# A two-layer fp32 encoder trunk on one Trainium2 core: the first feed-forward stage's down projection by seven products, its results added to x by transfers of 768 KB

## The chip, the core and the metric

The kernel runs on one core of one Trainium2 chip. Its engines are named here as the profile names them: PE is TensorE (PEld its weight loads), DVE is VectorE, ACT is ScalarE, POOL is GpSimd, SP is SyncE, which issues most loads. What counts is the device time of one execution in microseconds (us), as the median of several runs on the chip.

## The reference

Two sequences, a prompt of 512 tokens and a sample of 256, each token 1024 wide in fp32, go through a trunk of two layers. Each layer is a feed-forward block, a mixer and a second feed-forward block, each added to x after an RMS norm. The mixer of the first layer is an S5 state space (32 groups of 16 channels, 64 states, both directions) beside a neighbourhood attention, that of the second a windowed attention with grouped keys. The feed-forward block is

```python
def swiglu(x, wg, wu, wd):
    return (jax.nn.silu(x @ wg) * (x @ wu)) @ wd
```

with a hidden width of 2816, so 22 blocks of 128. The result is x after the last block, added with half weight per feed-forward block.

## The kernel before

**Stages.** `Trunk.run` goes through six stages: feed-forward 0, the mixer of layer 0, feed-forward 1 and 2, the mixer of layer 1, feed-forward 3. The 768 tokens lie in SBUF as six tiles of 128 x 1024 (`self.x`, in the order `TILES`, two of the sample and four of the prompt). Every fp32 operand of a matmul is split into a high and a low part (`split`, L86 to L90: ScalarE casts the high part, L89, VectorE subtracts it, L90), and a product takes three matmuls.

**Feed-forward, gate and up.** The 22 hidden blocks are taken in eleven pairs b. `quad` computes a pair's gate or up projection for both halves of the tokens by seven products after Strassen and Winograd instead of eight (`prod`, L283, twelve matmuls of 384 columns each); its weights are sums of quarter blocks that VectorE makes from the raw ones (`quad` in `weights`, L141 to L150). `up.use` multiplies gate and up (L354) and splits the result for the down projection.

**Feed-forward, down.** There are two forms. Stages 1 to 3 use `down` (L391): seven steps, each of three token tiles by nine matmuls of 512 columns, from sums of activations (L367 to L374) and sums of weights (L114 to L119). A step's three PSUM tiles go to x in one of two ways: VectorE adds them (L395), or ScalarE copies them to a buffer y (L398, five buffers) and GpSimd's queue issues a transfer of 256 KB that accumulates into x (L399). The steps are set between the products of the next pair by `woven`, one behind every second product. The first stage uses `plain` instead: twelve tiles of six matmuls of 512 columns (`rows`, L469), each added to x by VectorE (L416), all of them between the next pair's gate and up. The last pair of every stage is plain and lies in the stage's tail (`step`, L457), in which the next stage's norm (L230 to L232) is computed tile by tile.

**What sets the order.** The main loop at the end of `ffn` emits the steps one after another. Weights come in the order that the generator `weights.fast` lists them, at most `look` = 4 blocks ahead: SyncE loads a raw block of 512 KB (L80) into one of seven raw buffers, and ScalarE and VectorE split it into one of seven split buffers `whl`. There are eight PSUM tiles. In the first stage two of the raw buffers are held by `s5_matrices`.

**The S5 matrices** are made during the first stage, by a generator (`extra`) that is advanced once after each main step from the third pair on. For each of sixteen groups GpSimd computes two arrays w2 and w1 (L677 to L700, in `start`), `finish` stores w2 (L706), transposes w1 on TensorE (L711), lets ScalarE copy the transposed matrix to `w1e` (L712), whose memory is also GpSimd's scratch for the next group, and multiplies out a third one (L718 to L725); `store` sends w1e and that to DRAM (L729, L730) by GpSimd's queue.

## Time and profile before

| | us |
|---|---|
| median of 3 runs | 2641.65 (2640.74 to 2642.77) |
| the profiled execution | 2640.13 |
| its span in the trace | 2638.3 |
| TensorE busy | 2595.2 |
| VectorE busy | 2015.5 |
| ScalarE busy | 1545.2 |
| GpSimd busy | 769.1 |

The runs are timed without a profile; the trace belongs to the profiled execution, whose time and span differ by what lies around the program. Busy times count instructions that compute or issue transfers; an engine's idle time is charged by the profile to whatever released it. The first stage lasts up to about 550 us of the span; its first 76 us hold the first norm and the first pair's products, and the tail follows from 545 us.

### The profile page before, as it was taken

What the parts mean: (1) busy time and instruction counts of PE and PEld (TensorE: products, weight loads), DVE (VectorE), ACT (ScalarE), POOL (GpSimd) and SP (SyncE); (2) the same over time, 40 slices, a digit from 0 to 9 for tenths busy, and PEclk for the clock granted to TensorE, in tenths of its full rate; (3) what the DMA queues carried; (4) which work ended last, traced back from release to release, by engine and by line L of the source; (5) the groups of instructions that cost most, each with busy time, mean ns of one, the idle gap of its engine ahead of it and who ended that gap; (6) DMA issues with size and microseconds to landing.
All of it is one profiled execution on the core that took longest, in us unless ns stands there. A gap on an engine that the chain in (4) does not pass through costs nothing.

```text
span 2638.3 us, 40405 instructions
## 1 busy us (share of the span) xinstructions
PE 2595.2 (98%) x14370; PEld 2344.0 (89%) x14370; DVE 2015.5 (76%) x3925; ACT 1545.2 (59%) x3202; POOL 769.1 (29%) x1191
## 2 busy tenths in 40 slices
PE   8999999999999999999999999999999999999998
PEld 7999899888787899999998999999887789999997
DVE  8977777564864888787879878787647788878786
ACT  6334334354564666666667666666558766666665
POOL 0255655302820033333321323232100003333332
PEclk9999999999999999999999999999999999999999
DMA  4223223326243277777755877777401127777775
GB/s 154 71 90 104 78 91 104 106 74 155 82 155 108 88 168 165 171 166 170 167 108 137 190 169 167 168 170 148 128 17 41 65 88 168 165 171 166 170 167 129
DMA packets 145661, 342.92 MB, mean 130 GB/s; under 512 B 25265, under 2 KB 32385, under 8 KB 145202
## 3 DMA queue, kind: packets, MB, share of 16 engines
q0 software_dynamic: 74032, 139.01, 29.3%
q1 hardware_dynamic: 71426, 201.33, 23.7%
q8 instruction: 113, 1.85, 0.3%
q14 instruction: 90, 0.74, 0.1%
HBM read 198.65 MB, written 17.89 MB: 82 GB/s over the span
## 4 chain that ended last, share of the span: by engine, by line
PE 73%; DVE 4%; ACT 2%; DMA 1%; issue 1%; POOL 0%; DVEq 0%; ACTq 0%; POOLq 0%
PE ps L283 33%; PE ps L391 16%; PE ps L255 9%; PE ps L487 5%; PE ps L469 2%; PE ps L1111 1%; DVE whl L90 1%; PE ps L1099 1%; PE ps L1130 1%; DMA x<-y 1%; DVE raw L232 1%; PE ps L920 1%; PE ps L855 1%; PE ps L819 1%; PE ps L883 1%
## 5 line engine op out<-in xcount | busy, mean ns | idle before, releaser
L90 DVE TENSOR_TENSOR whl<-raw,whl 128x512 fp32r<-128x512 f32 x856 | 597.7, 704 | 346.7 <-ACT whl L89 337.1
L283 PE MATMUL ps<-bt,whl 128*128 128x384 f32 x4224 | 784.0, 337 | 14.6 <-ACT ct L315 5.8
L283 PEld LDWEIGHTS ps<-bt,whl 128*128 128x128 f32 x4224 | 742.0, 188 | 34.4 <-ACT ct L315 7.2
L89 ACT CAST whl<-raw 128x512 fp32r<-128x512 f32 x856 | 526.0, 621 | 327.5 <-issue 78.2
L399 POOL DMA_DIRECT2D x<-y x480 | 420.4, 1037 | 1009.9 <-ACT y L398 869.5
L283 PE MATMUL ps<-b,whl 128*128 128x384 f32 x3168 | 586.7, 336 | 3.6 <-ACT b L1294 2.9
L283 PEld LDWEIGHTS ps<-b,whl 128*128 128x128 f32 x3168 | 555.4, 188 | 14.4 <-ACT b L1294 3.3
L398 ACT ACTIVATE y<-ps 128x512 f32<-128x512 f32 x480 | 279.0, 598 | 67.7 <-PE ps L391 26.6
L391 PE MATMUL ps<-whl,hl 128*128 128x512 f32 x1080 | 269.8, 393 | 0.2 <-ACT hl L89 0.2
L391 PEld LDWEIGHTS ps<-whl,hl 128*128 128x128 f32 x1080 | 200.8, 188 | 36.7 <-ACT hl L89 0.5
L255 PE MATMUL ps<-hn,whl 128*128 128x256 f32 (+1 forms) x1248 | 228.7, 340 | 0.7 <-ACT hn L89 0.5
L255 PEld LDWEIGHTS ps<-hn,whl 128*128 128x128 f32 x1248 | 190.9, 190 | 29.3 <-issue 2.2
L391 PE MATMUL ps<-whl,h 128*128 128x512 f32 x810 | 202.9, 394 | 0.0
L469 PE MATMUL ps<-whl,h 128*128 128x512 f32 x756 | 191.1, 392 | 0.0
L391 PEld LDWEIGHTS ps<-whl,h 128*128 128x128 f32 x810 | 150.3, 188 | 28.2 <-ACT y L398 0.5
L469 PEld LDWEIGHTS ps<-whl,h 128*128 128x128 f32 x756 | 140.5, 188 | 30.1 <-ACT h L89 1.0
L89 ACT CAST h<-hct 128x384 fp32r<-128x384 f32 x132 | 67.8, 514 | 125.9 <-DVE hct L354 123.3
L89 ACT CAST whl<-st 128x512 fp32r<-128x512 f32 x118 | 72.8, 617 | 61.4 <-PE ps L469 39.9
L416 DVE SCALAR_TENSOR_TENSOR x<-ps,x 128x512 f32<-128x512 f32 x120 | 80.9, 685 | 34.4 <-PE ps L469 34.4
L395 DVE SCALAR_TENSOR_TENSOR x<-ps,x 128x512 f32<-128x512 f32 x150 | 99.9, 684 | 4.1 <-PE ps L391 4.1
L487 PE MATMUL ps<-whl,ob 128*128 128x512 f32 x432 | 102.5, 392 | 0.0
L90 DVE TENSOR_TENSOR whl<-st,whl 128x512 fp32r<-128x512 f32 x118 | 82.8, 701 | 22.3 <-ACT whl L89 20.8
(263 smaller groups left out, 3306.7 us busy)
## 6 DMA issues: line engine op xcount, KB each, us to landing
x<-y POOLq DMA_DIRECT2D x480, 256.0 KB, 5.2
raw<-in_w_gate SPq DMA_DIRECT2D x92, 512.0 KB, 5.5
raw<-in_w_up SPq DMA_DIRECT2D x92, 512.0 KB, 3.7
raw<-in_w_down SPq DMA_DIRECT2D x88, 512.0 KB, 5.3
raw<-in_w_in_even SPq DMA_DIRECT2D x16, 512.0 KB, 3.6
raw<-in_w_in_odd SPq DMA_DIRECT2D x10, 512.0 KB, 6.5
W2d<-raw POOLq DMA_DIRECT2D x16, 256.0 KB, 2.9
W1d<-hct POOLq DMA_DIRECT2D x16, 256.0 KB, 2.4
```

Of the source, the lines that this page charges most:

```text
L89: nc.scalar.copy(hl, src)
L90: nc.vector.tensor_sub(lo, src, hl.bitcast(F32))
L232: nc.vector.scalar_tensor_tensor(out[:, c], self.x[t][:, c], ss[:, 0:1], gb[:, c], ALU.mult, ALU.mult)
L255: self.nc.tensor.matmul(o, w[k // 4][:, j, k % 4 * P : (k % 4 + 1) * P], act[i][k // 4][:, k % 4, k0 : k0 + n], start=k == 0 and (j, i) == ...
L283: nc.tensor.matmul(o, w[:, j, k * P : (k + 1) * P], B[z][:, i, k], start=first and k == 0 and (j, i) == (0, 0), stop=k == 3 and (j, i) == ...
L391: nc.tensor.matmul(o, hs[h][:, c, n * P : (n + 1) * P], w[:, a], start=first and m == 0, stop=m == 2, skip_group_check=True)
L395: v.scalar_tensor_tensor(xs, o, 0.5, xs, ALU.mult, ALU.add)
L398: nc.scalar.activation(y, o, AF.Copy, scale=0.5)
L399: nc.gpsimd.dma_start(xs, y, accum_op=ALU.add)
L416: v.scalar_tensor_tensor(xs, o, 0.5, xs, ALU.mult, ALU.add)
L469: self.nc.tensor.matmul(o, act(f, i, n), w[:, j], start=f == 0 and (j, i) == (0, 0), stop=f == 1 and (j, i) == (0, 1))
L487: nc.tensor.matmul(o, act(i, k)[:, t * P : (t + 1) * P], st["w"][k][:, j], start=m == 0, stop=m == 11)
```

## The change

- x becomes one tile X of 128 x 6 x 1024; `self.x` are views of it.
- The first stage uses `down` for ten of its eleven pairs, woven as in the later stages; the step function `plain` is gone and only the tail's last pair stays plain. The sums of activations s1 to s4 and the split weights that go with them are now made in the first stage too. The buffers ct become four there (five elsewhere).
- In the first stage a step's three copies go to one buffer y of 128 x 3 x 512 (two of them), and one transfer of 768 KB adds them to x (L402 in the new file). The step that adds to the second token half's first column half still goes by VectorE.
- In the later stages the step s4 of the last woven pair adds by VectorE instead of ScalarE and a transfer.
- The transposed S5 matrix is copied back over its source w1 and stored from there, and two yields of the generator are gone, so a group takes eleven steps instead of thirteen.

```diff
@@ -60,7 +60,8 @@
         nc.vector.memset(warm, 1.0)
         nc.scalar.activation(warm, warm, AF.Sqrt)
         self.one = warm
-        self.x = [self.xp.tile([P, DM], F32, name=f"x{t}", tag=f"x{t}") for t in range(6)]
+        self.X = self.xp.tile([P, 6, DM], F32, name="x", tag="x")
+        self.x = [self.X[:, TILES.index(t)] for t in range(6)]
         self.queue = deque()
         self.look = 4
         self.stream = self.weights()
@@ -165,10 +166,7 @@
                 yield next(z)
             for b in range(1, NF // 2):
                 pair = [quad(n, q, b, b == 1) for n in both]
-                if q == 0:
-                    yield from chain(pair[0], plain(q, b - 1), pair[1])
-                else:
-                    yield from woven(b, chain(*pair), down(q, b - 1))
+                yield from woven(b, chain(*pair), down(q, b - 1))
             yield from plain(q, NF // 2 - 1)
 
         def out(n, kb, half):
@@ -272,7 +270,7 @@
             act = lambda f, i, n: hs[f"{n // 3 + 1}{f + 1}"][:, i, n % 3 * P : (n % 3 + 1) * P]
 
             def ct():
-                return fp.tile([P, H], F32, tag="ct", name="ct", bufs=5)
+                return fp.tile([P, H], F32, tag="ct", name="ct", bufs=5 if q else 4)
 
             def at(f, t):
                 return room[:, 0, 2 * f + t]
@@ -346,7 +344,7 @@
 
             def up(b):
 
-                last = b == NF // 2 - 1 or q == 0
+                last = b == NF // 2 - 1
                 sums = {}
 
                 def use(f, t, o):
@@ -383,6 +381,8 @@
 
                 def step(h, w, bank, first, i, j):
                     w = self.take("w_down", q, b, w)
+                    if q == 0 and (i, j) != (1, 0):
+                        y3 = fp.tile([P, 3, 512], F32, tag="y", name="y", bufs=2)
                     for n in range(3):
                         if first:
                             z[bank, n] = self.ps()
@@ -390,32 +390,21 @@
                         for m, (a, c) in enumerate(((0, 0), (1, 0), (0, 1))):
                             nc.tensor.matmul(o, hs[h][:, c, n * P : (n + 1) * P], w[:, a], start=first and m == 0, stop=m == 2,
                                              skip_group_check=True)
-                        xs = self.x[TILES[3 * i + n]][:, j * 512 : (j + 1) * 512]
-                        if (i, j) == (1, 0) or (i, j, n) == (0, 0, 0):
+                        xs = self.X[:, 3 * i + n, j * 512 : (j + 1) * 512]
+                        if (i, j) == (1, 0) or q and ((i, j, n) == (0, 0, 0) or h == "s4" and b == NF // 2 - 2):
                             v.scalar_tensor_tensor(xs, o, 0.5, xs, ALU.mult, ALU.add)
-                        else:
-                            y = fp.tile([P, 512], F32, tag="y", name="y", bufs=5)
-                            nc.scalar.activation(y, o, AF.Copy, scale=0.5)
+                            continue
+                        y = y3[:, n] if q == 0 else fp.tile([P, 512], F32, tag="y", name="y", bufs=5)
+                        nc.scalar.activation(y, o, AF.Copy, scale=0.5)
+                        if q:
                             nc.gpsimd.dma_start(xs, y, accum_op=ALU.add)
+                    if q == 0 and (i, j) != (1, 0):
+                        nc.gpsimd.dma_start(self.X[:, 3 * i : 3 * i + 3, j * 512 : (j + 1) * 512], y3, accum_op=ALU.add)
 
                 return [lambda s=s: step(*s) for s in (
                     ("11", "11", "b", True, 0, 0), ("s2", "t2", "b", False, 0, 1), ("s3", "t3", "b", False, 1, 1),
                     ("22", "t4", "b", False, 1, 0), ("12", "21", "a", True, 0, 0), ("s1", "t1", "c", True, 1, 1),
                     ("s4", "22", "c", False, 0, 1))]
-
-            def plain(b):
-
-                st = {}
-
-                def step(e, n):
-                    if n == 0:
-                        st["w"] = [self.take("w_down", q, 2 * b + f, e) for f in range(2)]
-                    o = self.ps()
-                    self.rows(o, act, n, st["w"])
-                    xs = self.x[TILES[n]][:, e * 512 : (e + 1) * 512]
-                    v.scalar_tensor_tensor(xs, o, 0.5, xs, ALU.mult, ALU.add)
-
-                return [lambda e=e, n=n: step(e, n) for e in range(2) for n in range(6)]
 
             def pair(b):
                 return quad("w_gate", b, gate), quad("w_up", b, up(b))
@@ -436,7 +425,7 @@
                     s()
             for b in range(1, NF // 2):
                 g, u = (z[2:] for z in (g1, u1)) if b == 1 else pair(b)
-                for s in g + plain(b - 1) + u if q == 0 else woven(b, g + u, iter(down(b - 1))):
+                for s in woven(b, g + u, iter(down(b - 1))):
                     s()
                     if b > 1:
                         next(extra, None)
@@ -676,7 +665,6 @@
             for r in range(2):
                 gp.tensor_mul(n1[:, r], b[:, r], crb)
                 gp.tensor_mul(n2[:, r], b[:, 1 - r], cib)
-            yield
             gp.tensor_sub(bb[:, 0, :2], n1[:, 0], n2[:, 0])
             gp.tensor_add(bb[:, 1, :2], n1[:, 1], n2[:, 1])
             gp.tensor_scalar(cn, c[:, 1], -1.0, None, ALU.mult)
@@ -698,7 +686,6 @@
             yield
             gp.tensor_mul(m2, cb_(bb[:, 1, :2]), pb_(P1, 0))
             gp.tensor_add(w1[:, :, 1], m1, m2)
-            yield
 
         def finish(q):
 
@@ -709,7 +696,7 @@
             w1f = w1.rearrange("p g r t c -> p (g r t c)")
             for e in range(4):
                 nc.tensor.transpose(pt[:, e * P : (e + 1) * P], w1f[:, e * P : (e + 1) * P], self.ident)
-            nc.scalar.copy(w1e, pt)
+            nc.scalar.copy(w1f, pt)
             pe, pf = self.ps(), self.ps()
             o, of = ([z[j * 32 : (j + 1) * 32] for j in range(2)] for z in (pe, pf))
             for j in range(2):
@@ -726,7 +713,7 @@
 
         def store(q):
             gs = slice(2 * q, 2 * q + 2)
-            nc.gpsimd.dma_start(self.W1d[:, gs, :], w1e.rearrange("p (g n) -> p g n", g=2))
+            nc.gpsimd.dma_start(self.W1d[:, gs, :], w1.rearrange("p g r t c -> p g (r t c)"))
             nc.gpsimd.dma_start(self.Ed[gs].rearrange("g c n -> (g c) n"), ee)
 
         load(0)
```

In TensorE's queue in the first stage, the last matmuls of a pair's plain down projection and the first products of the next pair's w_up (bt and b are the split norm outputs, whl the split weights, h and hl the split activations) stood, in the kernel before:

```order
L469 MATMUL ps<-whl,h_219 128x512 x21
L469 MATMUL ps<-whl,hl 128x512 x3
L469 MATMUL ps<-whl,h_219 128x512 x3
L469 MATMUL ps<-whl,hl 128x512 x3
L469 MATMUL ps<-whl,h_219 128x512 x3
L469 MATMUL ps<-whl,hl 128x512 x3
L469 MATMUL ps<-whl,h_219 128x512 x3
L283 MATMUL ps<-b_158,whl 128x384 x12
L283 MATMUL ps<-b_159,whl 128x384 x12
L283 MATMUL ps<-bt_250,whl 128x384 x12
```

and stand so now:

```order
L281 MATMUL ps<-bt_245,whl 128x384 x12
L281 MATMUL ps<-bt_244,whl 128x384 x12
L391 MATMUL ps<-whl,hl 128x512 x9
L281 MATMUL ps<-bt_501,whl 128x384 x12
L281 MATMUL ps<-b_548,whl 128x384 x12
L391 MATMUL ps<-whl,hl 128x512 x9
L281 MATMUL ps<-bt_604,whl 128x384 x12
L281 MATMUL ps<-b_153,whl 128x384 x12
L391 MATMUL ps<-whl,h_214 128x512 x9
```

The run of 72 matmuls (L469) is gone; nine matmuls of the down projection (L391) now follow every second product (L281, L283 before).

In GpSimd's queue, the end of an S5 group (L694 to L700, now L682 to L688, then the stores) was, before:

```order
L694 TENSOR_TENSOR hct<-s5k,raw 128x256
L706 DMA W2d<-raw 128x512
L696 TENSOR_TENSOR raw<-hct 128x2x128
L697 TENSOR_TENSOR hct<-s5k,raw 128x256
L699 TENSOR_TENSOR hct<-s5k,raw 128x256
L700 TENSOR_TENSOR raw<-hct 128x2x128
L729 DMA W1d<-hct 128x512
L663 DMA s5k<-in_s_bc 128x128
L730 DMA Ed<-hct 64x240
```

and is now:

```order
L682 TENSOR_TENSOR hct<-s5k,raw 128x256
L693 DMA W2d<-raw 128x512
L684 TENSOR_TENSOR raw<-hct 128x2x128
L685 TENSOR_TENSOR hct<-s5k,raw 128x256
L402 DMA x<-y 128x3x512
L687 TENSOR_TENSOR hct<-s5k,raw 128x256
L688 TENSOR_TENSOR raw<-hct 128x2x128
L666 TENSOR_TENSOR hct<-s5k 128x32
L667 TENSOR_TENSOR hct<-s5k 128x32
L666 TENSOR_TENSOR hct<-s5k 128x32
L667 TENSOR_TENSOR hct<-s5k 128x32
L402 DMA x<-y 128x3x512
```

The accumulating transfers (L402) now stand among the group's arithmetic, and the store of w1 (L716, before L729, then from w1e) stands behind the first operations of the next group (L666, L667).

On VectorE, in the first stage, the first reader of a w_up second half (raw_2683 on L141 before, raw_2294 on L142 now) and the split that gives its buffer free (of raw_2363 on L90 before, of raw_1967 on L91 now) stood before:

```order
L90 TENSOR_TENSOR whl_2477<-raw_2363,whl_2477 128x512
L90 TENSOR_TENSOR hl_647<-hct_218,hl_647 128x384
L354 TENSOR_TENSOR hct_218<-ps_2283,hct_218 128x384
L90 TENSOR_TENSOR whl_2496<-raw_2408,whl_2496 128x512
L90 TENSOR_TENSOR h3_219<-hct_218,h3_219 128x384
L90 TENSOR_TENSOR whl_2520<-raw_2516,whl_2520 128x512
L141 TENSOR_TENSOR st_2685<-raw_2683 128x512
```

and stand now:

```order
L91 TENSOR_TENSOR whl_2181<-raw_1967,whl_2181 128x512
L304 TENSOR_TENSOR hct_213<-ps_2141,hct_213 128x384
L91 TENSOR_TENSOR whl_2201<-raw_2039,whl_2201 128x512
L91 TENSOR_TENSOR whl_2221<-raw_1990,whl_2221 128x512
L142 TENSOR_TENSOR st_2296<-raw_2294 128x512
```

The distance between the two is six rows before and four now.

## Rows read from the trace of the kernel before

**Rows 1.** The page: busy time, share of the span and instructions of each engine.
```profile
PE 2595.2 (98%) x14370; PEld 2344.0 (89%) x14370; DVE 2015.5 (76%) x3925; ACT 1545.2 (59%) x3202; POOL 769.1 (29%) x1191
```

**Rows 2.** Stretches: length, busy PE, PEld, DVE, ACT, POOL, clock, DMA share, GB/s.
```profile
20.00:137.00 117.00, 114.13 (x602) 105.58 (x603) 113.67 (x273) 56.62 (x109) 13.75 (x19) 1.00 0.27 86
76.00:545.00 469.00, 462.99 (x2745) 425.94 (x2744) 353.03 (x621) 173.79 (x351) 222.97 (x365) 0.99 0.27 88
925.00:1355.00 430.00, 429.87 (x2259) 401.69 (x2258) 344.61 (x586) 277.36 (x535) 137.57 (x157) 1.00 0.77 167
545.00:565.00 20.00, 20.00 (x106) 16.69 (x105) 17.91 (x31) 13.58 (x36) 2.09 (x5) 1.00 0.26 80
```

**Rows 3.** TensorE's waits, 76 to 545 us: total, times, longest.
```profile
PE ps L283 <- ACT ct L315: 5.8, 1, 5.8
```

**Rows 4.** Timeline of TensorE, first stage: start, duration, instructions.
```profile
76.41 4.28 PE L469 MATMUL ps<-whl,h 128*128 128x512 f32 x18
...
92.77 6.43 PE L283 MATMUL ps<-bt,whl 128*128 128x384 f32 x36
99.04 2.24 PE L283 MATMUL ps<-b,whl 128*128 128x384 f32 x12
```

**Rows 5.** Timeline of TensorE, second stage, two steps of the down projection.
```profile
967.02 2.24 PE L391 MATMUL ps<-whl,h 128*128 128x512 f32 x9
...
973.28 2.24 PE L391 MATMUL ps<-whl,hl 128*128 128x512 f32 x9
```

**Rows 6.** Waits of SyncE's DMA queue, 76 to 545 us.
```profile
SPq L80 <- POOL hct L699: 20.4, 1, 20.4
```

**Rows 7.** VectorE's groups, 76 to 545 us: busy, mean ns, idle before, releasers.
```profile
L90 DVE TENSOR_TENSOR whl<-raw,whl 128x512 fp32r<-128x512 f32 x153 | 117.5, 769 | 29.7 <-ACT whl L89 26.6
L416 DVE SCALAR_TENSOR_TENSOR x<-ps,x 128x512 f32<-128x512 f32 x120 | 80.9, 685 | 34.4 <-PE ps L469 34.4
L90 DVE TENSOR_TENSOR h<-hct,h 128x384 fp32r<-128x384 f32 x29 | 19.1, 657 | 1.1 <-ACT h L89 0.6
L354 DVE TENSOR_TENSOR hct<-ct,hct 128x384 f32<-128x384 f32 x20 | 17.1, 854 | 0.0
L141 DVE TENSOR_TENSOR st<-raw 128x512 f32<-128x512 f32 x18 | 16.6, 922 | 16.1 <-DMA raw<-in_w_gate 8.2 <-DMA raw<-in_w_up 8.0
```

**Rows 8.** VectorE's groups, 925 to 1355 us.
```profile
L90 DVE TENSOR_TENSOR whl<-raw,whl 128x512 fp32r<-128x512 f32 x179 | 123.0, 689 | 76.0 <-ACT whl L89 74.7
...
L368 DVE TENSOR_TENSOR hct<-hct 128x384 f32<-128x384 f32 x10 | 5.6, 558 | 0.3
```

**Rows 9.** ScalarE's groups, 925 to 1355 us.
```profile
L89 ACT CAST whl<-raw 128x512 fp32r<-128x512 f32 x178 | 110.0, 619 | 47.3 <-issue 18.5 <-PE ps L283 17.6 <-PE ps L391 9.2
L398 ACT ACTIVATE y<-ps 128x512 f32<-128x512 f32 x157 | 91.0, 598 | 21.9 <-PE ps L391 8.5 <-DMA x<-y 8.0 <-ACT hct L342 0.2
```

**Rows 10.** GpSimd's accumulating transfers, whole kernel: issue ns min/median/max.
```profile
L399 POOL DMA_DIRECT2D x<-y x480: 852/887/1546, 929.5 to 2612.3; - x160
```

**Rows 11.** Timeline of GpSimd, 1348 to 1361 us.
```profile
1357.46 2.63 POOL L399 DMA_DIRECT2D x<-y  x3 [3.49 <-ACT y L398]
```

**Rows 12.** The same three transfers: issue ns, first and last start, landing.
```profile
L399 POOL DMA_DIRECT2D x<-y x3: 854/1042/1061, 1357.5 to 1359.0; - x3
...
DMA to landing us min/median/max: 3.3/4.2/4.6
```

**Rows 13.** VectorE's waits, 76 to 545 us.
```profile
DVE st L141 <- DMA raw<-in_w_gate: 8.2, 7, 1.4
```

**Rows 14.** DMA issues, 76 to 545 us: count, KB each, median us to landing.
```profile
raw<-in_w_gate SPq DMA_DIRECT2D x16, 512.0 KB, 3.8
```

**Rows 15.** DMA issues, 925 to 1355 us.
```profile
raw<-in_w_up SPq DMA_DIRECT2D x19, 512.0 KB, 3.7
raw<-in_w_gate SPq DMA_DIRECT2D x18, 512.0 KB, 6.4
```

**Rows 16.** The chain of waits, 540 to 575 us, in order of time.
```profile
550.62 0.37 DVE x L457
```

## The prediction

> **What bounds the kernel now.** I read the busy shares first: TensorE 98% of the span, VectorE 76%, ScalarE 59%, GpSimd 29% [rows 1]. So what shortens TensorE's own list can be gained, and what makes it wait is lost. Then the stretches [rows 2]. The first stage's main part (76 to 545 us, ten of its eleven pairs) is TensorE for 462.99 of 469.00 us, with 353.03 of VectorE, 173.79 of ScalarE and 222.97 of GpSimd. The second stage (925 to 1355 us) already runs the seven products that the first is to get: TensorE 429.87 of 430.00 with VectorE at 344.61 (80%). The opening (20 to 137 us, two of the ten pairs in it) is different: VectorE is busy 113.67 of 117.00 us, so only 3.3 are free. Last, TensorE's waits in the main part: one of 5.8 us [rows 3].
>
> A measurement of this kernel tells a difference over 0.2% (5.3 us) from no change. The profiled execution took 2640.1 us, 1.5 under the median of 2641.65; the sum is made against the former and 1.5 is added at the end.
>
> **TensorE, what is removed.** A pair's 72 matmuls of the plain down projection run from 76.41 to 92.77, 16.36 us, and 36 matmuls of products in a run from 92.77 to 99.04, 2.09 per twelve [rows 4]. So a pair is 14 × 2.09 + 16.36 = 45.62. Seven steps of nine take the place of the 72, each behind two products; from step to step it is 973.28 − 967.02 = 6.26 [rows 5], and a pair 7 × 6.26 = 43.82. The gain is 1.80 a pair, ten pairs: **−18.0**. The eleventh pair stays plain. With 2.09 a product the step itself is 2.08.
>
> **The one stall.** SyncE's queue stood 20.4 us behind a GpSimd operation of the S5 matrices [rows 6]: the raw buffer that S5 gives back went to a w_up load, and the 5.8 us of [rows 3] follow. In the new order that buffer goes to the norm gain, which only the tail reads. **−5.8**, with 0 as the other end if another load is late in its place.
>
> **VectorE.** Each pair loses nine additions to x (twelve to three) at 0.685 [rows 7]: −6.2. It gains three more weight splits (seven blocks for four), four operations to prepare the weights, four sums of activations and three more activation splits. At the first stage's prices (0.769, 0.922, 0.854, 0.657 [rows 7]) these are 2.3 + 3.7 + 3.4 + 2.0 = 11.4; at the second's (0.69 for 512 columns, 0.56 for 384 [rows 8]) 8.7. Net +2.5 to +5.2 a pair. The main part's 353 become 378 to 405 us of the 445 that are left of it (469.0 − 18.0 − 5.8): 85 to 91%. In the opening two pairs add 5.0 to 10.4, TensorE wants to be 3.6 earlier, 3.3 are free, so VectorE is 5.3 to 10.7 behind; weights split ahead can cover some or all of it. Between 0 and 10.7 I take **+4**, nearer the low end, since the part behind it has more slack.
>
> **ScalarE.** Eighteen copies to y a pair at 0.598, three more weight casts at 0.619 and three activation casts of at most that [rows 9]: 14.5 a pair, 174 + 145 = 319 of 445 us. No cost by itself.
>
> **GpSimd and the 768 KB transfers.** Sixty transfers in the main part. The trace has no accumulating transfer of this size. Below, an issue costs what one of 256 KB does, 0.85 us [rows 10]; above, what three do, 2.63 [rows 11]. So GpSimd goes from 223 to between 274 and 381 of 445 us. Landing: three of 256 KB land within 1359.0 + 4.6 − 1357.5 = 6.1 us of the first issue [rows 12]; the ends are 0.85 + 3.3 = 4.2 and 2.63 + 4.6 = 7.2. I take 6.1, the same bytes. A y buffer is wanted again two steps later, 2 × 6.26 less three copies: 10.7 us [rows 5, 9]. That holds unless S5's arithmetic is ahead in GpSimd's queue: a group of it is 223 / 16 = 13.9 us [rows 2], and in the new order a transfer stands within or right behind nearly every group. Half a group and the transfer make 7.0 + 6.1 = 13.1, so ScalarE is held 2.4 us. In the second stage ScalarE was held at the same place for 8.0 us in all [rows 9] while TensorE lost nothing.
>
> **The raw loads.** The new order on VectorE releases the buffer of each second half, of w_gate and of w_up, four rows before its first use; before, w_gate had four, w_up six. Four rows cost 8.2 us in seven waits, 1.2 each [rows 13], at loads that land in 3.8 us [rows 14]. Now the transfers bring traffic: 60 × 0.786 MB in 445 us is 106 GB/s on top of 88, more than the second stage's 167 [rows 2], where w_up lands in 3.7 us and w_gate in 6.4 [rows 15]. With the mean of these two, 5.1, a wait is 2.5; twenty are 50 us, and VectorE stands at 428 to 455 for 445. That is just at the edge, so single waits reach TensorE though the sum may fit. The ends are 0 and 36 (the slower rival). For loads and held copies together I take **+9**, the lower quarter, since the middle of 428 to 455 still fits.
>
> **The tail of the stage** is VectorE's: it is in the chain of waits [rows 16] and busy 17.91 of 20.00 us [rows 2]. The last transfer is issued some 0.7 us after step s4 and lands 4.2 to 7.2 later, so 4.9 to 7.9 after it. The first tile's second half wants that x after one product and twelve plain matmuls, 2.1 + 12 × 16.36 / 72 = 4.8 [rows 4]. VectorE waits 0.1 to 3.1 and has 2.1 free. At 6.1 the wait is 2.0; I take **+1.3**, with 0 and 3.1 as ends.
>
> The Trainium skill, "DMA: Bandwidth & Descriptors", section "Anatomy of one DMA — SWDGE (gpsimd) path", gives 2.0 us plus the bytes over 436e3; by it 768 KB would land in 3.8 us and this term would be 0. For 256 KB it gives 2.6, where the quickest row shows 3.3 [rows 12], so here the rows decide.
>
> **Edits at about nothing.** In the later stages three additions a stage go from ScalarE and GpSimd to VectorE, which is 80% busy there [rows 2]: 2.1 us shortly ahead of the tail against a transfer that no longer has to land; ±1, taken as 0. S5's matrix written back over its source and two fewer yields leave the same arithmetic off the path; the 187 steps that remain still fit the stage's 189. One tile for x: no operation changes.
>
> **Sum.** −18.0 − 5.8 + 4 + 1.3 + 9 = −9.5: 2640.1 − 9.5 + 1.5 = **2632 us**, chance 0.45, own range 2624 to 2640.
>
> **Rivals.**
> *VectorE becomes the bound (slower).* Place: the four-row release with five raw buffers, since S5 holds two. If both kinds of load go from 3.8 [rows 14] to the 6.4 of [rows 15], each wait grows by 2.6 to 3.8, twenty are 76 us, and VectorE needs 405 + 76 = 481 us for what took 469: +12, and +1.3 in the tail: 2655. It begins to bind at a mean wait of (445 − 405) / 20 = 2.0 us and makes the kernel slower by more than the bound above from (474 − 405) / 20 = 3.5. For it: the traffic, and 405 goes by the prices that the trace shows beside GpSimd's arithmetic, which goes on. Against: w_up's 3.7 us stood under nearly the same traffic, and some of VectorE's added work would fall into idle time that it spends on ScalarE now. Chance 0.25.
>
> *GpSimd hands the transfers over late (no change).* If an issue costs 2.63 us and each of sixteen S5 groups holds ScalarE, the weight casts behind the held copy are late, and if TensorE sees 0.6 of each of those 2.4 us, that is 10 more: 2642. For it: two y buffers where the second stage has five. Against: an issue's median of 0.887 stands close to its least of 0.852 with VectorE 80% busy [rows 2, 10], so nothing seems to hold GpSimd up there. Chance 0.17.
>
> The Trainium skill, "SBUF — State Buffer", section "SBUF: two separate sides", says that a VectorE operation holding the port pair that it shares with GpSimd keeps GpSimd from writing a transfer's descriptors, which would make this rival the likely one; by the issue times of [rows 10], the trace hardly shows it.
>
> *Everything is covered.* Nothing of the opening, the loads, the held copies and the tail reaches TensorE: −23.8, 2618. For it: the second stage, with the same steps, keeps TensorE busy for all but 0.13 us [rows 2]. Against: it has seven raw and five y buffers and no S5. Chance 0.13.
>
> That the plain projection stays is excluded for ten pairs by the new order: 63 matmuls a pair stand where 72 did.
>
> **How the numbers follow.** Faster by over 0.2% (under 2636.4) is most of the forecast's range and the full gain: 0.39 + 0.13 = 0.52. Within 0.2% lie the late transfers and the forecast's top: 0.17 + 0.06 = 0.23. Slower: 0.25. The range runs from just under the full gain to VectorE's bound: 2616 to 2655.
>
> **What would show it.** In the first stage a step's matmuls in runs of nine, 2.08 us each, between products of 2.09; no 5.8 us wait; VectorE 378 to 405 us busy there and ScalarE near 319; 60 GpSimd issues between 0.85 and 2.63 us; the waits for in_w_gate and in_w_up near 2.5 each. It is wrong if TensorE waits over 25 us in the main part (then the releaser, a weight split or a copy to y, names the rival), if the opening grows beyond 117 us, or if VectorE's prices go above [rows 7] beside the transfers.

## The result: 1.8% slower, and the profile after

| | before | after |
|---|---|---|
| median, us (4 runs each) | 2642.21 | 2688.95 (2684.89 to 2691.48) |
| ratio | | 1.0178, 95% interval 1.0166 to 1.0191 |
| first matmul of the mixer that follows the first stage, us | 564.82 | 608.93 |
| from there to the end of the span, us | 2073.5 | 2076.7 |

The forecast was 2632 us, with a range of 2616 to 2655. The kernel lost 47 us, and 44 of them by the end of the first stage. What follows is the profile of the changed kernel; in the new file the products are L281, the steps L391, the splits L90 and L91, the copies to y L398, the 768 KB transfer L402.

First the page's line of busy times; it answers to [rows 1].

```profile
PE 2601.0 (97%) x14280; PEld 2346.5 (87%) x14280; DVE 2067.4 (77%) x3984; ACT 1653.9 (62%) x3433; POOL 867.1 (32%) x1242
```

The stretches of [rows 2], now:

```profile
20.00:137.00 117.00, 109.95 (x579) 102.82 (x580) 113.19 (x277) 74.89 (x149) 21.17 (x24) 0.99 0.60 139
76.00:545.00 469.00, 426.09 (x2412) 388.91 (x2411) 375.03 (x633) 261.26 (x536) 304.59 (x398) 0.95 0.74 167
925.00:1355.00 430.00, 427.88 (x2270) 399.86 (x2269) 356.93 (x606) 281.90 (x552) 121.47 (x140) 1.00 0.73 163
545.00:565.00 20.00, 20.00 (x120) 18.38 (x119) 12.60 (x21) 12.58 (x27) 11.89 (x16) 0.93 0.96 213
```

In the first stage's main part TensorE fell from 462.99 to 426.09 us of 469, so it stands for 43 us of it, and its granted clock fell from 0.99 to 0.95. VectorE is busy 375.03, no more than 80%, ScalarE 261.26 and GpSimd 304.59: no engine is full. In the second stage TensorE waits 2.1 us of 430, with VectorE at 83%. The stretches end at fixed times, so for sums the next two rows are better: each runs from 60 us to the end of the first stage, first in the kernel before, then after.

```profile
60.00:565.00 505.00, 497.93 (x2930) 456.77 (x2930) 386.82 (x679) 198.23 (x407) 225.06 (x370) 0.99 0.27 89
```

```profile
60.00:609.00 549.00, 503.06 (x2846) 457.24 (x2844) 433.68 (x728) 312.46 (x647) 330.06 (x430) 0.95 0.74 166
```

505 us became 549. TensorE was busy 497.93 and is 503.06, where the forecast's 18 us less would have made 480; the other 46 are waits, where there were 7. In the main part they are these (releaser, total, times, longest); they answer to [rows 3].

```profile
PE ps L281 <- DVE ct L325: 21.5, 11, 4.8
PE ps L281 <- ACT hct L299: 10.0, 2, 5.6
PE ps L281 <- ACT whl L90: 4.9, 1, 4.9
PE ps L391 <- ACT y L398: 4.6, 1, 4.6
```

The single wait of 5.8 us for a late raw buffer is not among them; in its place are eleven waits for VectorE, 21.5 us (L325 adds up two products), and four for ScalarE, 19.5. VectorE's groups answer to [rows 7]: a weight split costs 0.836 us where it cost 0.769, and two operations of the weight preparation (L145 and L146, before L144 and L145) 1.054 and 0.885 where they cost 0.920 and 0.688. First now, then before:

```profile
L91 DVE TENSOR_TENSOR whl<-raw,whl 128x512 fp32r<-128x512 f32 x160 | 132.9, 836 | 42.0 <-ACT whl L90 40.4 <-PE ps L281 0.4
...
L145 DVE TENSOR_TENSOR raw<-raw 128x512 f32<-128x512 f32 x18 | 19.0, 1054 | 0.1
...
L146 DVE TENSOR_TENSOR raw<-st,raw 128x512 f32<-128x512 f32 x18 | 15.9, 885 | 0.2
```

```profile
L144 DVE TENSOR_TENSOR raw<-raw 128x512 f32<-128x512 f32 x18 | 16.6, 920 | 0.0
...
L145 DVE TENSOR_TENSOR raw<-st,raw 128x512 f32<-128x512 f32 x18 | 12.4, 688 | 0.3
```

VectorE's waits in the main part, for ScalarE's casts and, to be read beside [rows 13], for loads; ScalarE's wait for y over the whole stage, called a hold below; and the landing of the transfers (page) and of the two loads (76 to 560 us), with count, KB each and median us:

```profile
DVE whl L91 <- ACT whl L90: 42.1, 37, 8.8
DVE st L142 <- DMA raw<-in_w_up: 16.8, 6, 7.2
DVE st L142 <- DMA raw<-in_w_gate: 15.1, 8, 4.1
```

```profile
ACT y L398 <- DMA x<-y: 38.4, 11, 11.8
```

```profile
x<-y POOLq DMA_DIRECT2D x60, 768.0 KB, 7.2
```

```profile
raw<-in_w_gate SPq DMA_DIRECT2D x17, 512.0 KB, 5.3
raw<-in_w_up SPq DMA_DIRECT2D x18, 512.0 KB, 4.4
```

How these come together is seen between 160 and 190 us. GpSimd's timeline (start, duration, line, and in brackets the idle time before it and what ended it):

```profile
158.53 3.81 POOL L668 TENSOR_TENSOR s5k<-hct 128x32 f32<-128x32 f32 x1
...
176.24 1.35 POOL L402 DMA_DIRECT2D x<-y  x1
...
185.47 1.28 POOL L402 DMA_DIRECT2D x<-y  x1 [5.94 <-ACT y L398]
```

ScalarE's:

```profile
161.03 1.08 ACT L398 ACTIVATE y<-ps 128x512 f32<-128x512 f32 x2
...
183.01 0.60 ACT L398 ACTIVATE y<-ps 128x512 f32<-128x512 f32 x1 [11.82 <-DMA x<-y]
```

TensorE's, and its granted clock (the sixth figure behind the length, the counts in brackets left aside) in the two stretches of 5 us behind:

```profile
175.46 2.35 PE L281 MATMUL ps<-bt,whl 128*128 128x384 f32 x12 [1.24 <-DVE ct L325]
...
183.66 4.21 PE L391 MATMUL ps<-whl,h 128*128 128x512 f32 x9 [4.63 <-ACT y L398]
187.66 5.11 PE L281 MATMUL ps<-b,whl 128*128 128x384 f32 x24
```

```profile
180.00:185.00 5.00, 1.34 (x3) 1.15 (x4) 0.00 (x0) 1.99 (x5) 0.00 (x0) 0.75 1.12 189
185.00:190.00 5.00, 5.00 (x16) 4.32 (x16) 3.50 (x7) 3.72 (x9) 2.92 (x4) 0.56 0.93 159
```

The last two copies to a buffer y end at 162.1. Their transfer is issued at 176.24, because GpSimd works on an S5 group from 158.53 on that stands ahead of it in the queue, and it has landed at 183.0, 6.8 us later. There are two buffers, so the copy after the next waits 11.82 us for it, the weight casts and PSUM copies behind that copy wait with it, and TensorE stands for 4.63 us. Then the step's nine matmuls take 187.66 − 183.66 = 4.00 us in place of 2.08: the clock was granted at 0.56 of the full 2.4 GHz, near its lower level of 1.2. Just before it TensorE had only small matmuls of an S5 group and then stood. So a wait of TensorE is paid a second time.

This one event looks like the second rival (transfers handed over late). The sum of the stage is something else, as the experiments show.

### The profile page after: what moved, and what is told of

Same layout as the page of the kernel before. It is cut to its first block, busy times and chain, and to the rows that moved or that the text cites. A ratio compares the mean times of both kernels' runs of the same rounds, so it can differ in the third digit from the quotient of the medians.

```text
span 2685.6 us, 40643 instructions
## 1 busy us (share of the span) xinstructions
PE 2601.0 (97%) x14280; PEld 2346.5 (87%) x14280; DVE 2067.4 (77%) x3984; ACT 1653.9 (62%) x3433; POOL 867.1 (32%) x1242
## 4 chain that ended last, share of the span: by engine, by line
PE 79%; DVE 10%; DMA 3%; ACT 3%; issue 3%; POOL 2%; DVEq 0%; ACTq 0%; SPq 0%; POOLq 0%
PE ps L281 38%; PE ps L391 18%; PE ps L253 9%; PE ps L476 5%; DVE whl L91 3%; PE ps L458 1%; DMA x<-y 1%; PE ps L1098 1%; PE ps L1086 1%; DMA raw<-in_w_gate 1%; DVE raw L230 1%; DMA raw<-in_w_up 1%; ACT whl L90 1%; PE ps L1117 1%; PE ps L1256 1%
## 5 line engine op out<-in xcount | busy, mean ns | idle before, releaser
L91 DVE TENSOR_TENSOR whl<-raw,whl 128x512 fp32r<-128x512 f32 x876 | 623.8, 719 | 370.6 <-ACT whl L90 360.7
L281 PE MATMUL ps<-bt,whl 128*128 128x384 f32 x4224 | 798.1, 340 | 44.6 <-DVE ct L325 21.5
L281 PEld LDWEIGHTS ps<-bt,whl 128*128 128x128 f32 x4224 | 753.1, 191 | 70.0 <-DVE ct L325 25.7
L400 POOL DMA_DIRECT2D x<-y x471 | 413.1, 1038 | 996.4 <-ACT y L398 846.1
L90 ACT CAST whl<-raw 128x512 fp32r<-128x512 f32 x876 | 537.0, 622 | 258.4 <-PE ps L281 66.0
L281 PE MATMUL ps<-b,whl 128*128 128x384 f32 x3168 | 591.4, 337 | 4.8 <-ACT b L1281 2.9
L281 PEld LDWEIGHTS ps<-b,whl 128*128 128x128 f32 x3168 | 557.9, 188 | 18.3 <-ACT b L1281 3.3
L398 ACT ACTIVATE y<-ps 128x512 f32<-128x512 f32 x651 | 374.1, 598 | 115.2 <-DMA x<-y 59.8
L391 PE MATMUL ps<-whl,hl 128*128 128x512 f32 x1440 | 360.0, 394 | 0.2 <-ACT hl L90 0.2
L391 PEld LDWEIGHTS ps<-whl,hl 128*128 128x128 f32 x1440 | 268.2, 188 | 49.0 <-ACT hl L90 0.5
L391 PE MATMUL ps<-whl,h 128*128 128x512 f32 x1080 | 274.2, 398 | 4.6 <-ACT y L398 4.6
L391 PEld LDWEIGHTS ps<-whl,h 128*128 128x128 f32 x1080 | 203.3, 190 | 42.7 <-ACT y L398 4.7
L90 ACT CAST h<-hct 128x384 fp32r<-128x384 f32 x132 | 67.8, 513 | 137.7 <-DVE hct L352 137.6
L402 POOL DMA_DIRECT2D x<-y x60 | 79.2, 1336 | 177.9 <-ACT y L398 159.7
L395 DVE SCALAR_TENSOR_TENSOR x<-ps,x 128x512 f32<-128x512 f32 x189 | 125.4, 684 | 7.7 <-PE ps L391 7.6
L476 PEld LDWEIGHTS ps<-whl,ob 128*128 128x128 f32 x432 | 80.0, 188 | 18.4 <-issue 1.6
L91 DVE TENSOR_TENSOR whl<-st,whl 128x512 fp32r<-128x512 f32 x128 | 91.5, 715 | 3.4 <-ACT whl L90 1.9
L142 DVE TENSOR_TENSOR st<-raw 128x512 f32<-128x512 f32 x88 | 65.5, 744 | 36.1 <-DMA raw<-in_w_up 20.2
L90 ACT CAST whl<-st 128x512 fp32r<-128x512 f32 x128 | 79.0, 618 | 19.8 <-PE ps L281 14.8
```

The costliest lines, as they stand in the source:

```text
L90: nc.scalar.copy(hl, src)
L91: nc.vector.tensor_sub(lo, src, hl.bitcast(F32))
L142: v.tensor_add(s1, a21, a22)
L281: nc.tensor.matmul(o, w[:, j, k * P : (k + 1) * P], B[z][:, i, k], start=first and k == 0 and (j, i) == (0, 0), stop=k == 3 and (j, i) == ...
L391: nc.tensor.matmul(o, hs[h][:, c, n * P : (n + 1) * P], w[:, a], start=first and m == 0, stop=m == 2, skip_group_check=True)
L395: v.scalar_tensor_tensor(xs, o, 0.5, xs, ALU.mult, ALU.add)
```

## The experiments

Theory A, later called the queue theory: the transfers stand behind S5's arithmetic in GpSimd's queue. Theory B: VectorE is late, through its loads and its added work. Theory C: the size of the transfer. The neighbour theory came with e5: VectorE's operations are dearer beside GpSimd's arithmetic. Where no window is given, the waits below are those up to the end of the first stage or to 560 us. e3, e5 and e13 leave S5's arithmetic out for 15 of the 16 groups.

| run | edit to the changed kernel, unless it says before | median, us |
|---|---|---|
| e1_order | GpSimd's queue in program order | 2683.36 |
| e2_vector | no transfers in the first stage, VectorE adds all | 2666.99, one run |
| e3_no_s5 | no S5 arithmetic on GpSimd | 2631.77, one run |
| e4_small, e11_small_again | 256 KB transfers, six y | 2665.30, one run; 2669.90 |
| e5_memset | memsets in place of S5's arithmetic | 2641.39 |
| e6_small_order | e1 and e4 together | 2687.08 |
| e7_s5_only | before, with the S5 edits and VectorE's three additions | 2640.61 |
| e9_all_y | e4, no addition by VectorE | 2689.28 |
| e10_raw8 | e4 with four y and eight raw buffers | 2704.82 |
| e12_split | six pairs plain, S5 faster beside them | 2664.81 |
| e13_before_no_s5 | before, without S5's arithmetic | 2632.47 |
| e14, e15, e16 | eight, seven, six pairs plain, S5 at one step a main step | 2644.59, 2643.84, 2647.67 |

**GpSimd's order.**

```diff
-  gp.tensor_mul(m1, cb_(c[:, 0]), pb_(P2, 0))
+  self.pin(gp.tensor_mul(m1, cb_(c[:, 0]), pb_(P2, 0)))
...
-  nc.gpsimd.dma_start(self.X[:, 3 * i : 3 * i + 3, j * 512 : (j + 1) * 512], y3, accum_op=ALU.add)
+  self.pin(nc.gpsimd.dma_start(self.X[:, 3 * i : 3 * i + 3, j * 512 : (j + 1) * 512], y3, accum_op=ALU.add))
```

`pin` puts an instruction behind the one emitted before it on its engine.

> The changed kernel with one thing different: GpSimd's instructions of the S5 matrices and the 768 KB transfers keep the order in which the program emits them (two to three S5 steps between transfers, in place of whole groups of 14 us). Theory A (the transfers stand behind S5's arithmetic in GpSimd's queue, so y comes free late, ScalarE is held and the weight casts and PSUM reads behind it are late): ScalarE's waits for x<-y in the first stage fall from 38.4 us to under 15, TensorE's waits there from 58 to under 30, time 2625 to 2660. Theory B (VectorE is late because its weight preparation waits for the raw loads, 35 us, and it carries more work): nothing of that changes, 2680 to 2695.

Measured: 2683.36 us, ratio 1.0156 (1.0139 to 1.0173), 6 less than the change. The holds did fall, to 14.6 us, but TensorE's waits from 60 us to the end of the stage only from 46 to 41 (the 58 of the expectation count from the span's start), and a new one came: its transposes of w1 now wait for GpSimd.

```profile
PE ps L284 <- DVE ct L328: 14.3, 7, 3.2
PE ps L701 <- POOL raw L691: 11.4, 8, 3.3
```

```profile
ACT y L401 <- DMA x<-y: 14.6, 6, 4.8
```

The time lies in B's range and not in A's: 24 us of holds less gave 6 us. A fails as the whole story, and B's "nothing of that changes" fails too. The run is not a clean price of the holds, since some 11 us of what they gave went to the new wait.

**Without S5's arithmetic.**

```diff
             gp = nc.gpsimd
...
+            if q:
+                for _ in range(6):
+                    yield
+                return
```

> The changed kernel without GpSimd's arithmetic of the S5 matrices for 15 of the 16 groups (the arrays of the first group are stored again; so the output leaves that arithmetic out), everything else as it was, the loads, stores, transposes and copies too. Theory A: a transfer is issued within 1.5 us of its copies, ScalarE waits under 10 us for x<-y, time 2618 to 2635. Theory B: the raw loads and VectorE's added operations remain; VectorE's operations get cheaper where GpSimd's arithmetic stood beside them, 2660 to 2680.

Measured: 2631.77 us, within A's range and 28 below B's. The stage from 60 us to its end, and VectorE's splits in it:

```profile
60.00:553.00 493.00, 483.39 (x2841) 442.48 (x2840) 375.45 (x730) 314.42 (x648) 126.26 (x145) 0.99 0.82 185
```

```profile
L91 DVE TENSOR_TENSOR whl<-raw,whl 128x512 fp32r<-128x512 f32 x182 | 124.7, 692 | 76.6 <-ACT whl L90 75.6
```

The stage is 56 us shorter than in the change, and VectorE is busy 375.45 us for what took 433.68. But with the arithmetic two things went: the queue is free, and VectorE has no neighbour. The next run parts them.

**Memsets in the arithmetic's place.**

```diff
             gp = nc.gpsimd
+            if q:
+                def fill(z, *rest):
+                    for k in range(3 if math.prod(z.shape[1:]) > 200 else 2):
+                        nc.gpsimd.memset(w2[:, :, 0] if z is m1 or z is m2 else cn if z.shape[1:] == cn.shape[1:] else z, 0.001 * k)
+                gp = SimpleNamespace(tensor_mul=fill, tensor_add=fill, tensor_sub=fill, tensor_scalar=fill)
```

> The changed kernel with GpSimd's arithmetic of 15 of the 16 S5 groups replaced by memsets of about the same total length (the output leaves that arithmetic out): GpSimd is as long busy ahead of the transfers, but its instructions read nothing from SBUF. Queue theory (what costs is that the transfers stand behind GpSimd's work): ScalarE's waits for x<-y stay at 30 us or more and the time at 2670 or above. Neighbour theory (what costs is that VectorE's two-input operations run slower beside GpSimd's arithmetic, 0.836 us for a weight split in the changed kernel against 0.693 without it): the split falls to 0.72 or less and the time to 2632 to 2650.

Measured: 2641.39 us, ratio 1.0003 (0.9993 to 1.0013).

```profile
60.00:563.00 503.00, 484.68 (x2842) 442.23 (x2841) 371.90 (x728) 311.27 (x646) 296.10 (x895) 0.99 0.81 181
```

```profile
L92 DVE TENSOR_TENSOR whl<-raw,whl 128x512 fp32r<-128x512 f32 x182 | 124.8, 694 | 86.2 <-ACT whl L91 62.3 <-PE ps L392 20.4 <-PE ps L282 2.7
```

```profile
ACT y L399 <- DMA x<-y: 49.7, 20, 7.1
```

GpSimd is busy 296.10 us here and 330.06 in the change, so its queue is nearly as full, and ScalarE is held longer than in the change, 49.7 us against 38.4. The transfers and loads land no sooner as a whole (7.5 us, w_gate 4.4, w_up 5.4, against 7.2, 5.3 and 4.4). Still all of the 47 us lost are back. What changed is VectorE's price, 0.694 for a split against 0.828 over the same stage, and its waits for loads (11.2 us for w_gate, none for w_up). The change's line for the price, 60 to 609 us:

```profile
L91 DVE TENSOR_TENSOR whl<-raw,whl 128x512 fp32r<-128x512 f32 x182 | 149.6, 828 | 50.3 <-ACT whl L90 48.5 <-PE ps L281 0.4
```

The holds are covered when VectorE is quick. This is the neighbour theory's result. One rival is left by this run alone: a single hold is shorter here, 7.1 us at most against 11.8, so the few long ones could be what costs. The run with 256 KB transfers answers it below.

**The kernel before without the arithmetic** is the control.

> The kernel before without GpSimd's arithmetic for 15 of the 16 S5 groups (the output leaves it out). Neighbour theory: VectorE's prices fall here too (a weight split from 0.769 to about 0.69), but VectorE has idle time and the time stays within 8 us: 2633 to 2642. If S5's arithmetic costs both kernels the same: 57 us less, 2585.

Measured: 2632.47 us, ratio 0.9966 (0.9950 to 0.9981), half a us under the neighbour theory's range and far from 2585.

```profile
60.00:559.00 499.00, 497.21 (x2941) 456.88 (x2940) 361.05 (x683) 202.69 (x408) 48.57 (x85) 1.00 0.28 91
```

S5's arithmetic costs the first stage 6 us in the kernel before (505 against 499, the 5.8 us wait) and 56 in the changed one (549 against 493). It makes VectorE 386.82 − 361.05 = 26 us busier in the one and 433.68 − 375.45 = 58 in the other. Which operations get dearer can be read too. The additions to x, which take one operand from PSUM, cost the same with the arithmetic and without it: 0.685 [rows 7] and 0.687 in the kernel before, 0.681 in the change (60 to 609 us) and 0.683 in e5.

```profile
L416 DVE SCALAR_TENSOR_TENSOR x<-ps,x 128x512 f32<-128x512 f32 x120 | 82.2, 687 | 39.9 <-PE ps L469 39.8
```

```profile
L395 DVE SCALAR_TENSOR_TENSOR x<-ps,x 128x512 f32<-128x512 f32 x30 | 19.6, 681 | 3.4 <-PE ps L391 3.4
```

The splits and the weight preparation, with both operands in SBUF, are the ones that get dearer. The change takes 90 of the first kind from VectorE and gives it more of the second. And without the arithmetic the change gains only 499 − 493 = 6 us in the stage, not 18: TensorE is busy 14 less and waits 8 more.

**VectorE's load, taken away and added.**

```diff
-  if (i, j) == (1, 0) or q and (...):
+  if q == 0 or (i, j) == (1, 0) or (...):
...
```

> The changed kernel with all additions to x of the first stage by VectorE straight from PSUM: no y, no transfers there; VectorE gets 9 to 18 more additions a pair (about 18 x 0.685 = 12 us a pair, 120 in the stage) and ScalarE loses 18 copies (11 us a pair). Theory A: no hold by a transfer is left, but VectorE comes to about 495 us for 445, so it is the bound and the time is near 2690 to 2700, with the waits of TensorE on VectorE and none of ScalarE on x<-y. Theory B: VectorE, late already, is later by all of the 120 us: 2780 to 2810.

Measured: 2666.99 us in its one run, 22 less than the change and below both.

```profile
60.00:592.00 532.00, 490.48 (x2840) 441.54 (x2839) 514.21 (x909) 223.61 (x468) 259.10 (x370) 0.98 0.26 82
```

VectorE is 97% busy and is the bound here. So it can be filled when nothing on ScalarE is held by a transfer; in the change it stops at 79% and TensorE waits all the same. The transfers thus have a part in the loss: without them 22 us are back, although VectorE is busy for 514.21 us instead of 433.68 and a split still costs 0.788.

```diff
-  if (i, j) == (1, 0) or q and ((i, j, n) == (0, 0, 0) or ...):
+  if q and ((i, j) == (1, 0) or (i, j, n) == (0, 0, 0) or ...):
```

> The kernel with transfers of 256 KB and six buffers y, and besides all of a step's additions of the first stage by ScalarE and GpSimd: VectorE loses three additions a pair (20 us in the stage), ScalarE gains three copies and GpSimd three transfers a pair (30 issues of 0.9 to 1.0 us). If VectorE's time is the bound: 15 to 20 us less than with the transfers of 256 KB alone, 2645 to 2652. If the transfers and the y buffers are the bound: 5 to 15 us more, 2670 to 2680.

Measured: 2689.28 us, ratio 1.0182 (1.0168 to 1.0196), 19 above the kernel with 256 KB transfers alone and above both ranges. VectorE was relieved by 21 us in this stage (416.6 against 437.5), the holds rose from 10.2 to 25.7, and its waits for loads from 36.6 to 47.4 us:

```profile
DVE st L142 <- DMA raw<-in_w_gate: 25.7, 7, 5.6
DVE st L142 <- DMA raw<-in_w_up: 21.7, 7, 4.9
```

TensorE's waits for L325 rose from 21.9 to 36.2. So VectorE's busy time alone is not the bound either; the loads that it waits for land later beside more transfers (w_gate in 7.0 us instead of 5.6).

**The transfers' size.**

```diff
-  y3 = fp.tile([P, 3, 512], F32, tag="y", name="y", bufs=2)
...
+  y = fp.tile([P, 512], F32, tag="y", name="y", bufs=5 if q else 6)
...
+  nc.gpsimd.dma_start(xs, y, accum_op=ALU.add)
```

> The changed kernel with the first stage's additions as three transfers of 256 KB a step and six buffers y of 256 KB, the same room as the two of 768 KB. Theory A: the transfers still stand behind the S5 groups, and three issues of 0.9 to 1.0 us replace one of 1.3, so no better than 2680, perhaps 2700. Theory C (the size is what costs: a 768 KB transfer lands in 7.2 us and frees three tiles at once, a 256 KB one in 5.2 and frees its own): 2645 to 2670.

> The kernel with transfers of 256 KB and six buffers y once more, timed in rounds, since its one time (2665 us) stands apart from the kernels that are nearest to it (2683 to 2689). If the size of the transfer matters by itself: 2660 to 2670 again. If the one time was by chance: 2680 to 2690.

Measured: 2665.30 us once, then 2669.90, ratio 1.0106 (1.0091 to 1.0121). The interval lies apart from the change's: the 768 KB form costs 19 us against three transfers from the same room, with holds of 10.2 us in place of 38.4.

```profile
ACT y L396 <- DMA x<-y: 10.2, 6, 5.5
```

This bears on the rival from e5. No hold is longer than 5.5 us here, a split costs 0.843, as dear as in the change, and the kernel is still 1.06% or 28 us behind the kernel before. So without the long holds 19 of the 47 us are back and 28 are not, while e5, with quick operations, covers holds of 49.7 us in all.

> Both of the earlier edits at once: transfers of 256 KB with six buffers y, and GpSimd's queue in program order. Queue theory: what is left of the holds (13 to 15 us with either edit) goes to under 5, the time to 2640 to 2655. Neighbour theory: VectorE's prices stay, and the time stays at 2660 to 2672, the sum of the single edits not being reached.

Measured: 2687.08 us, ratio 1.0173 (1.0154 to 1.0191): program order took back all that the smaller transfers had given. TensorE waits 24.0 + 1.6 = 25.6 us for GpSimd's w1 over the stage. Neither theory had that. ScalarE is held for 0.3 us in all, so TensorE's other waits there have nothing to do with held copies.

```profile
PE ps L698 <- POOL raw L688: 24.0, 9, 4.9
```

```profile
ACT y L399 <- DMA x<-y: 0.3, 1, 0.3
```

> The changed kernel with transfers of 256 KB, four buffers y (in the later stages too) and, in the room that this frees, eight raw buffers instead of seven. VectorE's waits for the loads of w_gate and w_up in the first stage (33 us with 256 KB transfers and seven buffers) should fall to under 10. If those waits are a cost of their own: 20 to 30 us less than the kernel with 256 KB transfers. If they are only where VectorE's lateness shows (its prices beside GpSimd's arithmetic being the cause): less than 8 us better, or the waits come back as waits for ScalarE's casts.

```diff
-  r = self.wp.tile([P, 1024], F32, tag="raw", name="raw", bufs=7)
+  r = self.wp.tile([P, 1024], F32, tag="raw", name="raw", bufs=8)
...
-  y = fp.tile([P, 512], F32, tag="y", name="y", bufs=5 if q else 6)
+  y = fp.tile([P, 512], F32, tag="y", name="y", bufs=4)
```

Measured: 2704.82 us, ratio 1.0243 (1.0226 to 1.0260). The waits for loads went, to 3.1 us, and came back in another place.

```profile
DVE whl L91 <- ACT whl L90: 108.6, 56, 9.9
```

```profile
ACT y L396 <- DMA x<-y: 88.1, 44, 7.5
```

Holds of 88.1 us with four buffers, beside a VectorE that is late, are not covered. Some 10 us of this loss lie in the later stages, which have four y too, so the run doesn't price the loads; it shows that the y buffers can't pay for a raw one.

**The S5 edits without the seven products.**

> The kernel before with two edits of the change alone: the S5 matrix written back over its source with two yields fewer, and step s4 of the last woven pair of the later stages by VectorE; the first stage keeps the plain down projection. If the freed raw buffer no longer goes to a w_up load, TensorE's one wait of 5.8 us is gone and the time is 2634 to 2638; if another load is late in its place, or VectorE's additions delay the later stages' tails, 2640 to 2645.

Measured: 2640.61 us, ratio 0.9996 (0.9987 to 1.0005): no change. The wait of 5.8 us went and one of 5.0 came.

```profile
PE ps L283 <- DVE ct L327: 5.2, 2, 5.0
```

**Setting the two apart.**

```diff
+  early = q == 0 and b <= EARLY
+  for k, s in enumerate(g + plain(b - 1) + u if early else woven(b, g + u, iter(down(b - 1)))):
       s()
+      for _ in range((b > 1) * (1 + early * k % 2)):
+          next(extra, None)
```

> The changed kernel with the first six pairs of the first stage plain, as before, and the S5 steps taken three to every two main steps there, so that GpSimd's arithmetic is over before the last four pairs, which go by seven products and 768 KB transfers. Neighbour theory: the four pairs run without GpSimd's arithmetic, as in the second stage, and give 4 x 1.8 = 7 us; the denser S5 part costs nothing as long as VectorE has room beside the plain pairs: 2630 to 2638. If what costs is the transfers or the loads by themselves: the four pairs lose 4 of the 10 parts of the 47 us, 2655 to 2665. If the denser S5 part makes VectorE or TensorE wait: 2645 or more, with the loss in the first six pairs.

Measured: 2664.81 us, ratio 1.0085 (1.0070 to 1.0100). The neighbour theory's 2630 to 2638 is missed, and the time alone would also fit transfers that cost by themselves (2655 to 2665). The trace decides between them. The part with seven products and no arithmetic beside it does what was forecast: over 150 us TensorE waits 2.0 us.

```profile
400.00:550.00 150.00, 147.96 (x778) 137.97 (x777) 110.22 (x186) 94.41 (x184) 25.19 (x20) 1.00 0.84 179
```

```profile
PE ps L717 <- POOL raw L707: 14.4, 10, 2.9
```

The loss is in the first six pairs, where the denser S5 part makes TensorE's transposes wait for GpSimd. With S5 at its old pace (one step a main step) and `EARLY` at 8, 7 and 6:

> The changed kernel with the first eight pairs of the first stage plain and S5 at one step a main step, as in the kernel before, so that all of its arithmetic but 5 of 187 steps is over when the last two pairs go by seven products. Neighbour theory: the two pairs gain 1.8 us each against the plain first stage with the S5 edits (2640.6): 2635 to 2639. If seven products or their transfers cost something by themselves: 2 of 10 parts of the 47 us, 2648 to 2652.

> The same with seven pairs plain: 31 of the 187 S5 steps now lie beside seven products (a pair and a half), and one and a half pairs are free of them. Neighbour theory: a pair beside S5's arithmetic costs 4.9 us (the 44 us that the first stage grew, over its nine pairs with S5 steps), a free one gains 1.8: 2640.6 + 7.3 - 2.7, 2643 to 2648. If seven products cost by themselves, whatever is beside them: 2652 to 2657.

> The same with six pairs plain: 57 S5 steps (2.7 pairs) beside seven products, 1.3 pairs free. Neighbour theory: 2640.6 + 13.3 - 2.3, 2649 to 2654, above the kernel in which the same six pairs took all the S5 steps only if that one's waits of TensorE for GpSimd's w1 (16 us) cost less than this. If seven products cost by themselves: 2657 to 2662.

Measured: 2644.59 (ratio 1.0014, 1.0005 to 1.0023), 2643.84 (1.0010, 1.0001 to 1.0019) and 2647.67 us (1.0031, 1.0020 to 1.0042). With next to no pair beside S5's arithmetic (5 of 187 steps), one and a half, 2.7, and nine (the change), the time is 2645, 2644, 2648, 2689. e15 lies in its range, e16 1 us under its own. All three lie under the ranges for seven products that cost by themselves. The loss grows with the pairs that share their time with the arithmetic (and with the count of seven-product pairs, two, three, four and ten), for the first few by less than the 4.9 us a pair that were reckoned. That the free pairs bring a gain is not borne out: e14 missed its 2635 to 2639 by 5.6 us, with a wait of 4.3 us for a weight cast at its seven-product pairs. No version that keeps S5's arithmetic beats the kernel before; e7 equals it.

## Why the prediction was wrong, point by point

- **TensorE, −18.** The count was right (63 matmuls a pair, 2.08 us a step at full clock: e12's free part shows it). The 18 us did not show: without S5's arithmetic TensorE is 14 us less busy, and in the change 5 us more, at a granted clock of 0.95 in place of 0.99.
- **The stall, −5.8.** Gone, but by e7 another of 5.0 comes as soon as the order shifts. It was not a gain to count.
- **The opening, +4.** Between 20 and 137 us TensorE waits 117 − 109.95 = 7.0 us, before 2.9. The size came out right. The mechanism did not show: 4.9 us of it are one wait for a ScalarE weight cast, and e3 has the same 4.9 without the arithmetic.
- **VectorE's work.** The sum was nearly right: 386.8 us and the 25 to 52 added make 412 to 439 for the stage, measured 433.7. In part this is luck: without the arithmetic the added work is 375.45 − 361.05 = 14 us where at least 25 were reckoned, and what the arithmetic adds grew by 58 − 26 = 32 where at most (11.4 − 8.7) × 10 = 27 were. **The step that failed stands right behind the sum: the "85 to 91%" of the main part were taken as room enough, so that VectorE's work there got no term beyond the opening's, and loads and holds only a +9 for what just fails to fit.** It did not fit at 79%: TensorE waits 46 us in the stage where it waited 7. A share of busy time was set against the stage's length as if VectorE could use all that is left. It could not here: its splits wait for ScalarE's casts (42.1 us in the main part), its preparation for loads (31.9), and ScalarE in turn for VectorE (49.3 at the casts behind L352 alone) and for y (37.1).
- **The prices.** They were taken as constants of the first stage. They depend on what GpSimd does at the same time. The rows had it [rows 7, 8]: 0.769 beside the arithmetic, 0.689 without. The prediction used both as ends of a range and did not ask what the dearer one is made of, nor whether it holds for the new mix of operations (it became 0.836). By e5 this is the cause: with nearly as full a queue and the same transfers, but VectorE's prices down, 46 us of the stage are back. Of these, TensorE's waits are 45.9 − 18.3 = 27.6, and its slower matmuls 503.1 − 484.7 = 18.4.
- **Loads and held copies, +9 (0 to 36).** Mis-sized. The waits for loads came out near the forecast (2.3 us each for 2.5, fourteen for twenty), the holds at 38.4 us, eleven of 3.5 for the 2.4 reckoned. That they turn into TensorE's waits depends on VectorE's lateness: e5 covers 49.7 us of holds, the change does not cover 38.4. The dearer operations and the transfers act together: taking the dearness away gives all 47 us back, taking the transfers (e2) or their size (e4, e11) away gives 22 and 19. The slower matmuls behind the waits were in no term.
- **The transfers.** Issue 1.3 us (0.85 to 2.63 given), landing 7.2, at the upper end of 4.2 to 7.2. The queue ahead of the one shown at 160 us was 14 us, not the 7.0 of half a group.
- **The tail, +1.3.** From the first plain matmul to the mixer's first, 608.93 − 585.88 = 23.05 us against 564.82 − 544.85 = 19.97: +3.1, the upper end. VectorE waits 4.3 us for the last transfer.
- **Edits at about nothing.** From the mixer's first matmul to the end it is 2076.7 us in place of 2073.5; no run takes these 3 us apart, and e7, which has the edits of the later stages, shows no change of the time.
- **The rivals.** Two of the prediction's own signs of being wrong came: TensorE waits 43 us in the main part, over 25, and VectorE's prices lie above [rows 7]. The right sign was in the first rival, VectorE as the bound, but its condition was not met (loads at 6.4 us; they landed in 5.3 and 4.4 in the main part) and its 2655 was 34 short. The second's mechanism happens, as the 11.82 us show, and is not what decides. A split costs 0.828 us beside GpSimd's arithmetic, which reads SBUF, 0.694 beside memsets, which do not, and 0.692 with neither; an addition from PSUM costs 0.681 to 0.687 in all of them. The Trainium skill, "SBUF — State Buffer", section "SBUF: two separate sides", which the prediction drew on for another rule, says also that a VectorE operation with two SBUF inputs contends with a GpSimd one that reads SBUF, for one shared port pair. The runs agree with it.

Open: how much of the 46 us goes through the dearer operations themselves and how much through the holds and load waits that they leave uncovered; no run here slows VectorE alone.

## What to carry to other kernels

Before giving an engine more work, ask what its neighbour does in that stage and price the work there; a mean over the stage is the price at the present overlap and mix of operations, not at the new one. A busy share does not tell the room of an engine that waits for others: with VectorE at 80% TensorE waited 0.13 us in the second stage, with VectorE at 79% it waited 46 in this one. And count a wait of TensorE with the slower matmuls behind it.

## What was not expected of the hardware

- An accumulating transfer of 768 KB lands in 7.2 us at the median (up to 13.3), one of 256 KB in 5.3; its issue takes 1.29 us against 0.89.
- Behind a wait of 4.63 us TensorE's nine matmuls took 4.00 us instead of 2.08, and the clock was granted at 0.56 in the 5 us around them. Over the stage, against e5, such slower matmuls are 18 us beside 28 of waits.
- The same GpSimd arithmetic makes VectorE 26 us busier in one kernel and 58 in the other; the operations with both operands in SBUF get dearer, those that read PSUM do not (0.681 to 0.687 for an addition to x in both kernels, with the arithmetic and without).
